# Two-layer token-mixer and expert trunk: the second layer's input rows are scaled and shifted on GpSimd at another place

## The chip, the cores and the metric

One Trainium2 chip, of which the kernel uses one core. The metric is device time in microseconds (us) from start to end of one execution; lower is better. The engines of the core are TensorE (PE in the rows, with its weight loads as PEld), VectorE (DVE), ScalarE (ACT), GpSimd (POOL), and the DMA queues, of which SyncE's (SP) carries nearly all loads here.

## The reference

The batch is 1, the sequence 256 tokens, the width 1024, and there are two layers. Each layer ends both of its halves with a layer normalisation that has a scale row g and a shift row b:

```
mod = silu(c) @ w_ada[l] + b_ada[l]            # six parts: sh_m, sc_m, g_m, sh_f, sc_f, g_f
h   = x * (1 + sc_m) + sh_m
mix = token_mixers(h, w_in[l], w_out[l], ...)  # sparse attention, retention, mLSTM, then @ w_out
x   = layer_norm(alpha * x + (1 + g_m) * mix, ln_mix_g[l], ln_mix_b[l])
h   = x * (1 + sc_f) + sh_f
y   = moe_ffn(h, ...)                          # 16 experts, router, two experts for a token
x   = layer_norm(alpha * x + (1 + g_f) * y, ln_ffn_g[l], ln_ffn_b[l])

layer_norm(x, g, b) = (x - mean) * rsqrt(var + eps) * g + b
```

So the x that enters the second layer is needed twice: in h, ahead of the projections, and in `alpha * x`, behind w_out.

## The kernel before

**Tiles.** The tokens stand as two blocks of 128 on the partitions; a residual tile holds 128 x 2048 numbers (two blocks by 1024). One tile of tag X and three of tag H have that size. Weights come through a ring of ten 128x1024 buffers, rows such as g and b through two buffers of tag row.

**What one layer does.** The function `projections` multiplies h with w_in in eight parts, called projection 0 to 7 (0, the index part, is w_idx, 332 wide). Each goes over eight blocks k of 128 rows of the weight. Work in fp32 precision is done as three products of a high and a low part (`three`, L434 to L436); `wsplit` makes the parts of a weight block: ScalarE's cast (L415) and VectorE's subtraction with two SBUF inputs (L416; L426 has the same form for the first four blocks of projection 0). The parts lie in eight buffers of tag w, so four blocks at once. Between and behind the projections stand the attention's softmax, the convolution and gates of the mLSTM, and the retention's scores. The rope (L523 to L529) leaves one of its halves to GpSimd (L528) and the other to VectorE (L529).

**Places that the change touches.**
- The step between the layers (L880 to L895): the normalised rows xn of the first layer are transposed on TensorE, scaled and shifted by columns into the high part (ScalarE) and a second copy, and L888, a subtraction on VectorE, makes the low part of h. Beside it GpSimd's `affine_rows` (L459 to L466) makes the residual rows from xn: four multiplications by the g row (L463) and four additions of the b row (L464), each 128x512.
- The softmax: L633 on GpSimd divides by the sums.
- `make_aff` (L838): three VectorE operations of 128x8 (L841 to L843) that fold a norm's g and b columns into the modulation's scale and shift. Called ahead of the expert part with the name afff; L935 then makes a router weight of 128x128 from it. The modulation columns come from L406 and L411.
- The retention: scores (L716) into PSUM, masked by VectorE (L791, L792). L772 is the mLSTM's normalisation product, with one input in PSUM and one in SBUF; TensorE's scores wait for its result here.
- w_out is multiplied by (1 + g_m) on GpSimd (L917, 128x512), and split as above.
- L1039 fills the next residual tile with zeros on GpSimd.

**What sets the order.** The instructions of each engine are ordered by a scheduler ahead of time, from the program's order, priorities and dependences; `tc.issue_after(x)` holds an instruction behind x in that order. Loads go out on SyncE's queue in the order in which they are added to a list at the start (`Stream.add`), some 22 ahead of their use.

## Time and profile before

| | |
|---|---|
| Median of three runs | 730.05 us (729.27 to 730.53) |
| Profiled execution | 729.74 us |
| Span of the profile, first to last instruction | 728.0 us |
| Mean granted clock of TensorE | 0.957 of full speed |
| Busy share: TensorE, VectorE, ScalarE, GpSimd | 92%, 57%, 39%, 29% |

The busy share is an average over stages; the granted clock is that of TensorE, 1.00 for 2.4 GHz and 0.50 for 1.2 GHz. All rows of a trace come from the profiled execution.

### The profile page before, as it was taken

Reading aid. Unit: us, or ns where it says so; the run is one execution under the profiler, and the core shown is the slowest. Engines: PE = TensorE matmul, PEld = TensorE weight load, DVE = VectorE, ACT = ScalarE, POOL = GpSimd, SP = SyncE. Lnnn points to the kernel's source line nnn. Section 1 sums busy time; section 2 is a strip of 40 time slices with the busy share of each in tenths; the row PEclk is TensorE's granted clock in tenths of the full one; section 3 lists DMA queues with packets and bytes.
Section 4 is the critical chain, followed back from the end, with each engine's and each line's share of the span. In section 5 each row is a group of like instructions: output and inputs, shape, how many; then the busy total and the mean of one; then the engine's idle time right before and its main releaser. Section 6 shows DMA issues by size and latency. Waiting matters only on the chain. (4 is left out here: it accounts for less than half of the span.)

```text
span 728.0 us, 10437 instructions
## 1 busy us (share of the span) xinstructions
PE 667.6 (92%) x3638; PEld 409.9 (56%) x3638; DVE 414.1 (57%) x903; ACT 280.9 (39%) x583; POOL 208.2 (29%) x195
## 2 busy tenths in 40 slices
PE   5999699999898999999888999999899799999994
PEld 0567587864675434434347678885568554433431
DVE  5478986653975321243477999754645632234245
ACT  3346758344332212122256646944523212222131
POOL 3002933101913046102035613310740303712001
PEclk9999989999897999999998999999969789999998
DMA  8997773499986899999945773439958578999951
GB/s 305 407 368 241 258 267 112 144 363 409 377 299 236 310 322 349 370 408 407 365 156 172 235 256 116 144 125 319 396 183 276 187 264 304 354 353 407 406 193 58
DMA packets 57760, 204.19 MB, mean 280 GB/s; under 512 B 7336, under 2 KB 7464, under 8 KB 56422
## 3 DMA queue, kind: packets, MB, share of 16 engines
q1 hardware_dynamic: 55152, 198.49, 75.5%
q0 software_dynamic: 2112, 4.44, 1.6%
q8 instruction: 30, 0.49, 0.3%
q10 hardware_dynamic: 438, 0.54, 0.2%
q14 instruction: 28, 0.23, 0.1%
HBM read 202.15 MB, written 4.19 MB: 283 GB/s over the span
## 5 line engine op out<-in xcount | busy, mean ns | idle before, releaser
L416 DVE TENSOR_TENSOR sb_w<-sb_ring,sb_w 128x512 fp32r<-128x512 f32 (+1 forms) x156 | 117.1, 764 | 42.6 <-ACT sb_w L415 40.6
L415 ACT CAST sb_w<-sb_ring 128x512 fp32r<-128x512 f32 (+1 forms) x156 | 92.1, 608 | 89.0 <-PE ps_mm L435 44.2
L1208 PE MATMUL ps_s<-sb_ring,sb_S 128*64 128x512 f32 x424 | 116.2, 600 | 0.2 <-PEq L1117 0.2
L435 PE MATMUL ps_mm<-sb_w,sb_H 128*128 128x512 f32 (+2 forms) x224 | 79.9, 359 | 4.3 <-DVE sb_H L888 4.3
L434 PE MATMUL ps_mm<-sb_w,sb_H 128*128 128x512 f32 (+2 forms) x224 | 80.2, 365 | 1.9 <-ACT sb_w L415 1.3
L436 PE MATMUL ps_mm<-sb_w,sb_H 128*128 128x512 f32 (+2 forms) x224 | 74.9, 369 | 0.7 <-DVE sb_w L416 0.6
L917 POOL TENSOR_TENSOR sb_ring<-sb_ring,sb_g 128x512 f32<-128x512 f32 x32 | 45.5, 1460 | 72.0 <-DMA sb_ring<-w_out 70.8
L1208 PEld LDWEIGHTS ps_s<-sb_ring,sb_S 128*64 128x64 f32 x424 | 32.5, 136 | 54.0 <-issue 45.9
L349 PE MATMUL ps_t<-sb_ring,cact 128*32 128x512 f32 x272 | 47.7, 616 | 7.8 <-DVE posf L296 6.2
L434 PEld LDWEIGHTS ps_mm<-sb_w,sb_H 128*128 128x128 f32 x224 | 43.0, 194 | 10.7 <-ACT sb_w L415 2.8
L435 PEld LDWEIGHTS ps_mm<-sb_w,sb_H 128*128 128x128 f32 x224 | 43.3, 194 | 10.1 <-DVE sb_H L888 5.0
L436 PEld LDWEIGHTS ps_mm<-sb_w,sb_H 128*128 128x128 f32 x224 | 41.7, 194 | 11.6 <-issue 3.8
L1107 DVE TENSOR_SCALAR sb_S<-ps_t,afffg,afffb 128x256 f32<-128x256 f32 x32 | 17.4, 543 | 48.9 <-ACT sb_S L210 48.4
L1099 PEld LDWEIGHTS ps_t<-sb_O,sb_H 128*128 128x128 f32 x256 | 33.1, 193 | 19.9 <-issue 11.4
L1256 PE MATMUL ps_t<-sb_P,sb_sg 128*64 128x512 f32 x152 | 42.4, 599 | 0.5 <-ACT sb_sg L1243 0.5
L528 POOL TENSOR_TENSOR sb_rope<-sb_rope 128x256 f32<-128x256 f32 (+1 forms) x16 | 15.8, 990 | 89.3 <-DVE iwm L564 31.5
L435 PE MATMUL ps_mm<-sb_H,sb_w 128*128 128x256 f32 x128 | 37.3, 292 | 3.9 <-DVE sb_w L416 3.9
L1099 PE MATMUL ps_t<-sb_O,sb_H 128*128 128x256 f32 x256 | 39.0, 297 | 2.0 <-DVE sb_O L1029 1.8
L633 POOL TENSOR_SCALAR sb_sg<-sb_sg,sm 128x128 f32<-128x128 f32 (+1 forms) x32 | 26.6, 847 | 45.5 <-DVE sm L630 23.3
L210 ACT ACTIVATE sb_S<-ps_t,afffb,afffg 128x256 f32<-128x256 f32 x32 | 18.0, 563 | 55.9 <-PE ps_t L1099 55.1
L434 PE MATMUL ps_mm<-sb_H,sb_w 128*128 128x256 f32 x128 | 37.1, 291 | 0.0
L436 PE MATMUL ps_mm<-sb_H,sb_w 128*128 128x256 f32 x128 | 36.9, 288 | 0.0
(369 smaller groups left out, 1234.1 us busy)
## 6 DMA issues: line engine op xcount, KB each, us to landing
sb_ring<-w_gu SPq DMA_DIRECT2D x106, 512.0 KB, 7.4
sb_ring<-w_ada SPq DMA_DIRECT2D x96, 512.0 KB, 6.9
sb_P<-w_dn SPq DMA_DIRECT2D x58, 512.0 KB, 7.9
sb_ring<-w_in SPq DMA_DIRECT2D x56, 512.0 KB, 6.1
sb_ring<-w_out SPq DMA_DIRECT2D x16, 512.0 KB, 10.1
sb_S<-w_gu SPq DMA_DIRECT2D x6, 1024.0 KB, 8.4
sb_row<-rows SPq DMA_DIRECT2D x8, 512.0 KB, 9.6
sb_w<-w_gu SPq DMA_DIRECT2D x12, 256.0 KB, 4.7
```

The costliest lines, as they stand in the source:

```text
L210: return A.activation(o, i, f, bias=bias, scale=scale)
L349: PE.matmul(pa[32 * g:32 * g + 32, :], cact[:, k:k + 1].to_broadcast([P, 32]), w[g // 2][:, (g % 2) * 512:(g % 2) * 512 + 512], start=(i = ...
L415: A.copy(hi, src)
L416: V.tensor_tensor(lo, src, hi.bitcast(F32), op=OP.subtract)
L434: PE.matmul(o, a[0], b[0], start=start, stop=False)
L435: PE.matmul(o, a[1], b[0], start=False, stop=False)
L436: return PE.matmul(o, a[0], b[1], start=False, stop=stop)
L633: G.tensor_scalar(sg[:, i * n:(i + 1) * n], sg[:, i * n:(i + 1) * n], sm[:, h:h + 1], None, op0=OP.mult)
L917: G.tensor_tensor(q, q, g1[l][0][:, n * 512:(n + 1) * 512], op=OP.mult)
L1099: last = PE.matmul(pt[:, j * 256:(j + 1) * 256], src[:, tt * D + k * P:tt * D + (k + 1) * P], oh[:, tt * D + q * 256:tt * D + (q + 1) * 25 ...
L1208: PE.matmul(pgu[s * 64:s * 64 + 64, :], xg[:, c0:c0 + 64], ws[s][k], start=(i == order[0] and k == 0), stop=(i == order[3] and k == 1), ti ...
L1256: PE.matmul(pyb[s * 64:s * 64 + 64, :], hdT[:, k, s * 64:s * 64 + 64], wd[s][k], start=(k == 0), stop=(k == 1), tile_position=(0, 64 * s))
```

## The change

In the second layer the residual rows are no longer made at the step between the layers. The normalised rows xn stay in their H tile, and the eight operations of `affine_rows` work in place on it later, behind the softmax's last GpSimd operation (`behind.soft`), issued with projection 5. Their two row loads move in SyncE's list from ahead of w_idx to behind projection 5. The tile that the convolution uses is taken from X in the second layer, and from H in the first as before. Apart from that, in both layers `make_aff` for the expert part is issued behind the last masked retention score (`projections.scored`).

```diff
--- before.py
+++ after.py
@@ -153,13 +153,13 @@
                     st.add(("in", l, n), chunk(l, n), which=(i,))
         for la, na in EARLY[l]:
             st.add(("ada", la, na), w_ada[la, na])
-        if l:
-            norm_rows(2 * l - 1)
         for n in range(8):
             if l or n > 1:
                 st.add(("in", l, n), chunk(l, n))
             for la, na in LATER[l].get(n, ()):
                 st.add(("ada", la, na), w_ada[la, na])
+            if l and n == 5:
+                norm_rows(2 * l - 1)
         norm_rows(2 * l)
         for n, which in ((0, (0, 1)), (1, (0, 1)), (0, (2,)), (1, (2,)), (0, (3,)), (1, (3,))):
             st.add(("out", l, n), w_out[l, n], which=which)
@@ -505,6 +505,9 @@
             if l == 0 and n == 5:
                 with tc.issue_after(st.last.ins):
                     nc.sync.dma_start(xres, x_tok)
+            if l and n == 5:
+                with tc.issue_after(behind.soft.ins):
+                    affine_rows(xres, xres, 2 * l - 1)
             while pending:
                 modulation(*pending.pop(0), ones, "t")
             for la, na in LATER[l].get(n, ()):
@@ -630,7 +633,7 @@
                     V.reciprocal(sm[:, h0:h1], sm[:, h0:h1])
                     for i in range(per):
                         h = h0 + i
-                        G.tensor_scalar(sg[:, i * n:(i + 1) * n], sg[:, i * n:(i + 1) * n], sm[:, h:h + 1], None, op0=OP.mult)
+                        behind.soft = G.tensor_scalar(sg[:, i * n:(i + 1) * n], sg[:, i * n:(i + 1) * n], sm[:, h:h + 1], None, op0=OP.mult)
                     pt = ps("t")
                     for j in range(4):
                         PE.transpose(pt[:, j * P:(j + 1) * P], sg[:, j * P:(j + 1) * P], ident)
@@ -687,7 +690,7 @@
         for k, w in blocks(3):
             cols_part(k, wsplit(w), [pm[j // 2][:, (j % 2) * 256:(j % 2) * 256 + 256] for j in range(4)])
         behind(3)
-        cvs = sb("H").rearrange("p (i j t) -> p i j t", i=2, j=4)
+        cvs = sb("X" if l else "H").rearrange("p (i j t) -> p i j t", i=2, j=4)
         cv, sg = cvs[:, 0], cvs[:, 1]
         mq = sb("S")
         mqk = mq[:, 0:1024].rearrange("p (h t) -> p h t", h=4)
@@ -789,7 +792,7 @@
         rv = sdb[:, 1536:2048].rearrange("p (t d) -> p t d", t=2)
         for h, pq in scores(rqk[:, 0:2, :], rqk[:, 2:4, :]):
             V.tensor_tensor(sd[h][:, 0:256], pq[:, 0:256], dec[:, h, :], op=OP.mult)
-            V.tensor_tensor(sd[h][:, 256:384], pq[:, 256:384], dec[:, h, 0:128], op=OP.mult)
+            projections.scored = V.tensor_tensor(sd[h][:, 256:384], pq[:, 256:384], dec[:, h, 0:128], op=OP.mult)
         pv = ps("mm")
         pv = [pv[:, tt * 256:(tt + 1) * 256] for tt in range(2)]
         pgt = ps("mm")
@@ -891,8 +894,8 @@
                 with tc.issue_after(moved.ins):
                     A.copy(a, sums)
                 modulation(la, na, a, quad, "t", True)
-            xres = sb("X")
-            affine_rows(xres, xn, 2 * l - 1)
+
+            xres = xn
 
         oT = projections(l, hT, inputs)
 
@@ -929,7 +932,8 @@
 
         ws = [(n, j, out_w(n, j)) for n in range(2) for j in (6, 7)]
         st.ahead = AHEAD + 8
-        gp, bp = make_aff(par_("lnm_g")[:, l * 8:l * 8 + 8], par_("lnm_b")[:, l * 8:l * 8 + 8], modc[l][:, 3, :], modc[l][:, 2, :], "afff")
+        with tc.issue_after(projections.scored.ins):
+            gp, bp = make_aff(par_("lnm_g")[:, l * 8:l * 8 + 8], par_("lnm_b")[:, l * 8:l * 8 + 8], modc[l][:, 3, :], modc[l][:, 2, :], "afff")
 
         wrg = wk.tile([P, KD, E], F32, name="wrg", tag="wrg")
         V.tensor_tensor(wrg, wr, gp[:, :, None].to_broadcast([P, KD, E]), op=OP.mult)
```

The next rows give, for one engine each, the program's order of instructions ("x4" is a run of four). On **GpSimd**, second layer, from the end of the expert part of the first layer to w_out's scaling (L453 is a statistic of the norm, L380 a sum for the modulation). A piece of the difference at the step between the layers (rows with a minus stood there before):

```order
 L1161 DMA sb_H<-table_117,which 128x1024 x2
 L453 TENSOR_SCALAR mr<-mv,rs 128x1 x2
-L463 TENSOR_TENSOR sb_X<-sb_H,sb_row 128x512 x4
-L464 TENSOR_TENSOR sb_X<-sb_X,sb_row 128x512 x4
 L380 TENSOR_TENSOR sb_a<-sb_a,sb_ring 128x512 x4
 L531 TENSOR_TENSOR sb_rope<-sb_rope 128x5x32
```

and one behind the softmax (rows with a plus stand there now; lines are numbered 3 to 4 higher after the change, so L636 is L633, L531 is L528, L920 is L917 and L1043 is L1039):

```order
 L636 TENSOR_SCALAR sb_sg<-sb_sg,sm 128x128 x8
 L636 TENSOR_SCALAR sb_sg<-sb_sg,sm 128x256 x8
+L463 TENSOR_TENSOR sb_H<-sb_H,sb_row 128x512 x4
+L1043 MEMSET sb_X 128x2048
+L464 TENSOR_TENSOR sb_H<-sb_H,sb_row 128x512 x4
 L531 TENSOR_TENSOR sb_rope<-sb_rope 128x8x32 x2
 L920 TENSOR_TENSOR sb_ring<-sb_ring,sb_g_3715 128x512 x16
-L1043 MEMSET sb_X 128x2048
```

The eight row operations moved from behind the norm to behind the softmax, work on sb_H in place, and have the zero fill of the next sb_X between them; the rope's halves of projection 5 stand behind them.

On **VectorE**, second layer, at the retention's scores. Before:

```order
L406 TENSOR_REDUCE mod<-ps_t 128x4
L411 TENSOR_TENSOR modc_269<-mod,bada 128x2x2
L841 TENSOR_TENSOR afffg<-pr,modc_269 128x8
L842 TENSOR_TENSOR afffb<-pr,modc_269 128x8
L772 TENSOR_TENSOR sb_e<-ps_s,sb_e 128x512
L935 TENSOR_TENSOR wrg<-pr,afffg 128x128
L843 TENSOR_TENSOR afffb<-afffb,modc_269 128x8
L791 TENSOR_TENSOR sb_S<-ps_s,dec 128x256
L792 TENSOR_TENSOR sb_S<-ps_s,dec 128x128
L791 TENSOR_TENSOR sb_S<-ps_s,dec 128x256
L792 TENSOR_TENSOR sb_S<-ps_s,dec 128x128
```

and now (L772 in it is L769 of before; the product that was L772 is L775 and stands four rows further up, straight behind L411):

```order
L795 TENSOR_TENSOR sb_S<-ps_s,dec 128x128
L772 TENSOR_TENSOR sb_O<-sb_e,sb_O 128x512
L794 TENSOR_TENSOR sb_S<-ps_s,dec 128x256
L795 TENSOR_TENSOR sb_S<-ps_s,dec 128x128
L794 TENSOR_TENSOR sb_S<-ps_s,dec 128x256
L795 TENSOR_TENSOR sb_S<-ps_s,dec 128x128
L844 TENSOR_TENSOR afffg<-pr,modc_269 128x8
L845 TENSOR_TENSOR afffb<-pr,modc_269 128x8
L939 TENSOR_TENSOR wrg<-pr,afffg 128x128
L846 TENSOR_TENSOR afffb<-afffb,modc_269 128x8
L416 TENSOR_TENSOR sb_w<-sb_ring,sb_w 128x512 x4
```

The three operations of `make_aff` and the router product moved from both sides of L772 (now L775) to behind the last masked score, ahead of the splits of w_out.

On **VectorE**, first layer (affmg and affmb are the parts for the step to the second layer, which have stood among the retention's scores already). Before, ahead of the mLSTM's scores:

```order
L406 TENSOR_REDUCE mod<-ps_t 128x4
L411 TENSOR_TENSOR modc_268<-mod,bada 128x2x2
L841 TENSOR_TENSOR afffg<-pr,modc_268 128x8
L842 TENSOR_TENSOR afffb<-pr,modc_268 128x8
L935 TENSOR_TENSOR wrg<-pr,afffg 128x128
L843 TENSOR_TENSOR afffb<-afffb,modc_268 128x8
L721 TENSOR_TENSOR sb_P<-ps_s,sb_P 128x384
```

and now, at the end of the retention's scores:

```order
L795 TENSOR_TENSOR sb_S<-ps_s,dec 128x128
L845 TENSOR_TENSOR affmb<-pr,modc_269 128x8
L794 TENSOR_TENSOR sb_S<-ps_s,dec 128x256
L795 TENSOR_TENSOR sb_S<-ps_s,dec 128x128
L844 TENSOR_TENSOR afffg<-pr,modc_268 128x8
L845 TENSOR_TENSOR afffb<-pr,modc_268 128x8
L846 TENSOR_TENSOR affmb<-affmb,modc_269 128x8
L939 TENSOR_TENSOR wrg<-pr,afffg 128x128
L846 TENSOR_TENSOR afffb<-afffb,modc_268 128x8
L416 TENSOR_TENSOR sb_w<-sb_ring,sb_w 128x512 x4
```

The afff operations left the place between two L721 and stand between those of affm, directly ahead of the splits of w_out.

On TensorE the order changes at one place of the stretch: in the second layer the transposes of the rope's result of projection 5 (L785) stand eight to eighteen matmuls of the next projections later.

## Rows read from the trace of the kernel before

**Rows 1.** The page, busy us, share of the span and instructions of each engine:

```profile
PE 667.6 (92%) x3638; PEld 409.9 (56%) x3638; DVE 414.1 (57%) x903; ACT 280.9 (39%) x583; POOL 208.2 (29%) x195
```

**Rows 2.** Timeline of GpSimd, 330 to 640 (start us, length, operation, idle before):

```profile
375.93 5.68 POOL L463 TENSOR_TENSOR sb_X<-sb_H,sb_row 128x512 f32<-128x512 f32 x4 [0.32 <-DVE sb_H L1289]
381.57 5.84 POOL L464 TENSOR_TENSOR sb_X<-sb_X,sb_row 128x512 f32<-128x512 f32 x4
...
463.83 4.75 POOL L633 TENSOR_SCALAR sb_sg<-sb_sg,sm 128x256 f32<-128x256 f32 x4 [2.53 <-DVE sm L630]
478.65 1.58 POOL L528 TENSOR_TENSOR sb_rope<-sb_rope 128x256 f32<-128x256 f32 x1 [10.08 <-DVE rowz L661]
...
566.51 1.80 POOL L1039 MEMSET sb_X<- 128x2048 f32 x1 [30.40 <-DVE sb_H L835]
```

**Rows 3.** VectorE's groups, 375.9 to 387.4 (count, busy us, mean ns, idle before):

```profile
L888 DVE TENSOR_TENSOR sb_H<-sb_h,sb_H 128x256 fp32r<-128x256 f32 x4 | 5.3, 1342 | 0.0
L426 DVE TENSOR_TENSOR sb_w<-sb_ring,sb_w 128x332 fp32r<-128x332 f32 x4 | 5.2, 1288 | 0.0
```

**Rows 4.** VectorE's groups, 388 to 394:

```profile
L416 DVE TENSOR_TENSOR sb_w<-sb_ring,sb_w 128x332 fp32r<-128x332 f32 x4 | 2.0, 493 | 0.0
L888 DVE TENSOR_TENSOR sb_H<-sb_h,sb_H 128x256 fp32r<-128x256 f32 x4 | 1.7, 421 | 0.1
```

**Rows 5.** TensorE's waits, 374 to 400 (total us, times, longest):

```profile
PE ps_mm L435 <- DVE sb_H L888: 4.3, 2, 2.4
```

**Rows 6.** Windows: length, then busy us (count) by engine; granted clock last but two:

```profile
382.00:388.00 6.00, 3.55 (x13) 3.17 (x12) 6.00 (x5) 1.63 (x4) 5.41 (x4) 0.50 0.32 111
...
468.00:482.00 14.00, 14.00 (x101) 12.65 (x99) 12.98 (x26) 7.18 (x13) 3.12 (x3) 1.00 0.66 217
482.00:488.00 6.00, 6.00 (x50) 5.53 (x49) 0.00 (x0) 3.99 (x10) 0.00 (x0) 1.00 0.05 21
526.00:538.00 12.00, 10.76 (x26) 7.38 (x28) 6.39 (x13) 1.75 (x3) 10.11 (x8) 0.50 0.53 193
```

**Rows 7.** Timeline, second layer's retention scores, 518 to 548:

```profile
523.55 1.02 DVE L411 TENSOR_TENSOR modc<-mod,bada 128x4 f32<-128x4 f32 x1
524.61 1.19 DVE L841 TENSOR_TENSOR afffg<-pr,modc 128x8 f32<-128x8 f32 x1
...
525.80 0.68 DVE L772 TENSOR_TENSOR sb_e<-ps_s,sb_e 128x512 f32<-128x512 f32 x1
...
526.53 1.65 PE L716 MATMUL ps_s<-sb_S 64*128 64x256 f32 x4 [2.88 <-DVE sb_e L772]
527.08 1.22 DVE L843 TENSOR_TENSOR afffb<-afffb,modc 128x8 f32<-128x8 f32 x1
...
528.89 1.64 PE L716 MATMUL ps_s<-sb_S 64*128 64x256 f32 x4 [0.71 <-DVE sb_S L792]
```

**Rows 8.** Timeline of VectorE, first layer, 138 to 215:

```profile
151.55 0.17 DVE L841 TENSOR_TENSOR afffg<-pr,modc 128x8 f32<-128x8 f32 x1
...
187.25 1.82 DVE L416 TENSOR_TENSOR sb_w<-sb_ring,sb_w 128x512 fp32r<-128x512 f32 x1
```

**Rows 9.** VectorE's groups, first layer's w_out stretch, 179.4 to 204:

```profile
L416 DVE TENSOR_TENSOR sb_w<-sb_ring,sb_w 128x512 fp32r<-128x512 f32 x8 | 11.6, 1458 | 0.6 <-ACT sb_w L415 0.6
```

**Rows 10.** Timeline of TensorE, projection 6 of the second layer:

```profile
471.61 0.75 PE L436 MATMUL ps_mm<-sb_w,sb_H 128*128 128x512 f32 x3
...
477.71 0.28 PE L436 MATMUL ps_mm<-sb_w,sb_H 128*128 128x256 f32 x1
```

**Rows 11.** Timeline of VectorE, 455 to 500:

```profile
469.97 1.27 DVE L416 TENSOR_TENSOR sb_w<-sb_ring,sb_w 128x512 fp32r<-128x512 f32 x2
...
474.59 0.67 DVE L416 TENSOR_TENSOR sb_w<-sb_ring,sb_w 128x512 fp32r<-128x512 f32 x1
...
479.24 0.40 DVE L529 TENSOR_TENSOR sb_rope<-sb_rope 128x256 f32<-128x256 f32 x1
```

**Rows 12.** Timeline of TensorE, first layer's w_out stretch, 176 to 216:

```profile
190.81 1.02 PE L436 MATMUL ps_mm<-sb_w,sb_O 128*128 128x512 f32 x2
```

## The prediction

> **What bounds the kernel now.** Lines are those of the kernel before (the same lines stand 3 or 4 further down after the change). I read the page first: TensorE is busy for 92% of the span and no other engine for more than 57% [rows 1], so time is gained or lost where TensorE waits or runs at the lower clock. The change touches four stretches, and I looked at each by its own view.
>
> At the step between the layers GpSimd runs the eight row operations of the scale and shift from 375.93 to 387.41 [rows 2]. In that stretch VectorE's subtractions with two SBUF inputs take 1342 and 1288 ns [rows 3]; the same shapes take 421 and 493 ns just behind it [rows 4]. TensorE waits 4.3 us for those subtractions [rows 5], and from 382 to 388 it runs at 0.50 of the clock, 1.2 GHz [rows 6].
>
> Behind the softmax, from 468 to 482, TensorE is busy 14.00 of 14.00 us at full clock and VectorE 12.98 of 14, while GpSimd works 3.12 us [rows 6]. This is where the row operations go: free for GpSimd, full for the two others.
>
> At the retention scores of the second layer VectorE's tiny operations take about 1.2 us each while GpSimd scales w_out, and TensorE waits 2.88 us for the operation behind them [rows 7]. TensorE then runs at 0.50 until 538 [rows 6]. In the first layer the same tiny operations stand in a quiet place, at 0.17 us [rows 8].
>
> **The change part by part.** All four sums use one mechanism, which the rows show: while GpSimd runs a chain of operations with SBUF inputs, a VectorE operation with two SBUF inputs gets in about once per GpSimd operation, whatever its size. In the w_out stretches 128x8 elements cost 1.19 us [rows 7] and 128x512 cost 1.46 us on average [rows 9], while L772, which has one input in PSUM, stays at 0.68 us there [rows 7]. I call one turn a slot, of 1.46 us (5.84 for four GpSimd operations [rows 2]).
>
> *Step between layers.* Eight GpSimd operations leave. VectorE's eight subtractions there shrink by 4 x (1.342 - 0.421) + 4 x (1.288 - 0.493) = 6.9 us [rows 3, 4]. TensorE's 4.3 us of waiting should mostly go [rows 5], and of its 3.55 us busy at half clock half is saved, 1.8 us [rows 6]: 6.1 together. Next in line are ScalarE's two activations for each block, which TensorE and VectorE also need, so some waiting stays, about 1 us as I estimate from following the chain with the short durations. I take a gain of 5.0. Bounds: 6.9, all of VectorE's saving; and 3.0, the wait less 1.3 for what ScalarE holds back, with the clock falling all the same. The two row loads leave the queue ahead of w_idx; nothing waited for that queue here, so I price it at nothing; if it did count, it would be a gain of the two issues.
>
> *Behind the softmax.* The softmax's last GpSimd operation ends at 468.58 [rows 2]. Then come four multiplications, the zero fill of the next residual tile (1.80 us, now between them [rows 2]) and four additions: 8 x 1.46 + 1.80 = 13.5 us, to about 482.1. Counted along VectorE's order, the operations with two SBUF inputs are: the last split of projection 5, one gate operation, the splits of blocks 0 and 1 of projection 6 (slots 1 to 4); the splits of blocks 2 and 3 (under the fill); two gate operations and the split of block 4 (slots 5 to 7). Block 0 is then split by 468.58 + 3 x 1.46 + 0.67 = 473.6. TensorE wants it with the third matmul of the row at 471.61, about 472.0 [rows 10]; before, it was there ahead of that, being the first of the pair at 469.97 [rows 11]. TensorE waits 1.6 us. Block 4 is split by 468.58 + 4 x 1.46 + 1.80 + 3 x 1.46 + 0.67 = 481.3 in place of 475.26 [rows 11]; TensorE wants it at 477.71 [rows 10], now 479.3: another 2.0. After that GpSimd is done and VectorE catches up, as it is idle from 482 to 488; TensorE is not, 6.00 of 6.00 [rows 6], so what it lost stays lost. The loss is 3.6 us. Bounds: 1.0, if the splits are far enough ahead for most of it; 7, if a fall of the clock comes on top (the second rival).
>
> The fill is priced as if it did not contend. No row shows a fill beside such a VectorE operation. If it took slots like a reader, blocks 2 and 3 would be late too, by at most one slot on the path, 1.5 us; if it does not, nothing. I take nothing, since L772 shows that it is the second SBUF read that is held up [rows 7], and a fill reads nothing. The Trainium skill, page "SBUF — State Buffer", section "Who interferes with whom", says the same outright: a VectorE instruction with two SBUF inputs contends with a GpSimd instruction that reads SBUF and not with one that only writes. By that rule the loss here is the 3.6 of the slots; by a rule that all GpSimd work contends it would be 5.1, and the sum below -0.6 in place of -2.1. No row of this trace decides it.
>
> Queued behind the row operations on GpSimd is the rope's half for projection 5, which started at 478.65 [rows 2] and now starts about 3.5 us later. TensorE's transposes wait for it; the new order puts them behind eight to eighteen more matmuls, and TensorE itself is 3.6 late by then, so I add nothing. Without that cover it would be up to 3.5 us. The row loads now go out between the weights of projections 5 and 6, so ahead of weights that are already split at 469.97 [rows 11]; the next row loads, which need the same two buffers, go out only behind the weights of projection 7. No wait for either. The convolution's tile moves from H to X, which is free since the residual was folded in near the end of the first layer: no wait. The fill leaves its place ahead of the token split, where GpSimd had stood idle for 30.40 us before it [rows 2]; what follows it there can only come earlier: nothing.
>
> *Affine parts, second layer.* L411 ends at 524.57. L772 could start then, but starts at 525.80 behind L841 (1.19) [rows 7]. Without those it starts 1.2 us earlier, and TensorE's scores at 526.53 come at 525.3. The next scores, at 528.89, waited for L791 and L792, which stood behind L843 (1.22, from 527.08) and the router product [rows 7]; they now follow at once, at about 527.0. With the bank that the last scores need free as well, TensorE is 2.4 us ahead by then (1.2 + 0.7 of the second wait + about 0.5 of the third). The four operations themselves go behind the last score, where VectorE next waits for ScalarE: free. Gain 2.4. Bounds: 1.2, the first wait alone; 4.3, if the stretch at half clock gets shorter too.
>
> *Affine parts, first layer.* The same four leave a quiet place (0.17 us, [rows 8]) for one inside the w_out stretch, directly ahead of the split at 187.25 [rows 8]. In the second layer they took slots of 1.19 and 1.22 [rows 7], and two more squeezed into the same gaps; here I take two slots less the gap they fill, 2.5 us. The split that ended at 189.07 then ends at 191.6, and TensorE wants it at 190.81 [rows 12]: 0.8 of waiting at first, up to 2.5 where later operations in the chain have no slack. I take a loss of 1.7, the middle. Bounds: 0 and 4.8 (four at 1.19).
>
> **Sum.** -5.0 + 3.6 - 2.4 + 1.7 = -2.1 us. The profiled execution took 729.74 us (span 728.0 and 1.7 around it), 0.3 below the median of 730.05; its sum gives 727.6, and against the median 728.0.
>
> **Rivals.**
> *The window hides more* (T = 725.4): the splits run far enough ahead and the loss behind the softmax is 1.0. For it: eight buffers hold four pairs, and beside a single GpSimd operation, the rope's half at 478.65, VectorE's L529 took 0.40 while GpSimd's took 1.58 [rows 2, 11], so it can be GpSimd that is held up. Against: the row operations come in chains of four, as at the step, and the split of block 0 is only about one block ahead of its use [rows 10, 11]. Sum -5.0 + 1.0 - 2.4 + 1.7 = -4.7.
> *Slower: the clock falls behind the softmax* (T = 732). Two waits of 1.6 and 2.0 us in a stretch that was gapless. At the step, waits of 4.3 in all were followed by the lower clock [rows 5, 6], and in 526 to 538 TensorE was busy 10.76 us at 0.50 [rows 6]. A fall to 1.2 GHz costs half of the busy time it lasts. It makes the change slower than before by 0.2% from 3.6 us of loss on, which is 7 us at the lower clock; for 8 us it costs 4.0 and the sum is +1.9. Against it: the two waits are five us apart with dense work between.
> *The step gives less* (T = 730.0): ScalarE's activations or the lower clock hold the step; the gain is 3.0, the sum -0.1. For it: ScalarE is the next in that chain. It is also the case in which the move does not do what it is for.
>
> **How the numbers follow.** Forecast 0.52, window hidden 0.13, clock falls 0.20, step gives less 0.15. Within 0.2%, 1.46 us, a measurement of this kernel can hardly tell a difference from none. Faster: most of the forecast (0.43) and the hidden window (0.13): 0.56. Slower: most of the third case, 0.18. Same: the rest, 0.26. The range reaches from below the hidden window, 724.8, to inside the slower case, 731.6; the forecast alone would be 726.0 to 729.4.
>
> **What would show it.** Right: at the step L888 near 0.42 us, no wait of TensorE over 1 us, full clock; behind the softmax L416 near 1.5 us and two waits of TensorE for it, 3 to 4 us in all; in the second layer's scores the product of L772 straight behind L411 and the wait down to about 1.7; in the first layer four operations of 0.2 to 1.2 us ahead of the split. Wrong: granted clock below 1 between 470 and 490; TensorE waiting at the step for ScalarE; a wait of TensorE for GpSimd's rope.

## The result

The changed kernel took 723.17 us (median of 20 runs, 718.45 to 727.46) against 728.2 us for the kernel before (median of 20, 726.15 to 733.25). The ratio is 0.9927, with a 95% interval of 0.9906 to 0.9947: 5.3 us faster, 3.9 to 6.9. The direction was as forecast; the size forecast was 2.1 us. The median lies below the stated range (724.8). Some of that is the reference: the three runs of the kernel before that were shown had a median of 730.05, the twenty have 728.2. The rest, 5.3 in place of 2.1 us, is the change itself. The ratios here and below leave out runs that lie more than 1.5% above the fastest of their kernel: three of twelve in r4, one of six in r13, and one of the 17 of the kernel before beside r12 to r14.

The profile after, for the lines that answer to [rows 1, 2, 5]. The page, busy us and share of the span by engine; GpSimd's timeline from 455 to 495; TensorE's waits from 374 to 400; and a window at the step (columns as in [rows 6]):

```profile
PE 669.7 (92%) x3638; PEld 407.6 (56%) x3638; DVE 414.8 (57%) x903; ACT 280.5 (39%) x583; POOL 212.5 (29%) x195
```

```profile
467.57 8.51 POOL L463 TENSOR_TENSOR sb_H<-sb_H,sb_row 128x512 f32<-128x512 f32 x4
476.02 1.81 POOL L1043 MEMSET sb_X<- 128x2048 f32 x1
477.79 7.51 POOL L464 TENSOR_TENSOR sb_H<-sb_H,sb_row 128x512 f32<-128x512 f32 x4
485.26 0.90 POOL L531 TENSOR_TENSOR sb_rope<-sb_rope 128x256 f32<-128x256 f32 x1
```

```profile
PE ps_mm L434 <- ACT sb_H L210: 0.6, 1, 0.6
PE ps_mm L436 <- DVE sb_w L416: 0.6, 1, 0.6
PE ps_mm L435 <- DVE sb_H L891: 0.5, 1, 0.5
```

```profile
382.00:388.00 6.00, 4.92 (x31) 4.23 (x32) 5.37 (x13) 5.92 (x14) 0.00 (x0) 1.00 0.97 370
```

The page hardly moves. At the step the 4.3 us of waiting for VectorE's subtractions [rows 5] are down to 0.5, the two other waits are short (0.6 each), and TensorE has the full clock. Behind the softmax the row operations take 8.51 and 7.51 us for four, where they took 5.68 and 5.84 at the step [rows 2], and the rope's half starts at 485.26.

**Lengths of stretches.** To compare many kernels I measured each stretch between two landmarks that all have: the ends of VectorE's 160 splits of weights from the ring (L416 and L426), numbered from 0 in its order. The names r1 to r14 are those of the experiments below. *First w_out* is from split 62 to 78, *step* from 80 to 84, *softmax* from 126 to 136, *scores* (second layer, with half of its w_out) from 136 to 152, and *last* from split 158 to the end of the span. In us, from one profile each:

| Kernel | First w_out | Step | Softmax | Scores | Last | Span |
|---|---|---|---|---|---|---|
| before | 46.9 | 10.5 | 31.1 | 52.6 | 168.1 | 728.0 |
| before, again (r8) | 45.9 | 10.5 | 31.4 | 52.2 | 168.1 | 728.5 |
| changed | 49.6 | 4.9 | 35.3 | 47.2 | 167.7 | 725.6 |
| changed, again (r1) | 50.1 | 4.9 | 35.2 | 47.1 | 166.5 | 723.8 |
| changed, third (r11) | 49.6 | 4.9 | 35.1 | 48.8 | 166.8 | 722.2 |
| r2 rows only | 46.8 | 4.9 | 34.6 | 51.4 | 166.7 | 721.3 |
| r3 rows, second affine | 45.9 | 4.9 | 35.3 | 47.5 | 166.7 | 719.4 |
| r4 affine only | 49.6 | 10.5 | 31.1 | 48.2 | 168.0 | 727.0 |
| r9 second affine only | 45.9 | 10.5 | 31.1 | 46.3 | 169.0 | 721.9 |
| r10 first affine only | 49.6 | 10.5 | 31.5 | 51.1 | 169.1 | 729.7 |
| r12 second fill late | 45.8 | 10.5 | 31.6 | 52.1 | 167.0 | 723.5 |
| r5 rows behind rope | 46.7 | 4.9 | 31.3 | 45.5 | 166.8 | 712.8 |
| r6 rows left out | 45.8 | 4.9 | 31.7 | 47.5 | 166.9 | 716.1 |
| r7 one input | 45.8 | 4.9 | 32.4 | 42.5 | 166.5 | 710.8 |

Mean of the changed kernel's three profiles less the mean of the two of before: +3.4, -5.7, +4.0, -4.7 and -1.1, together -4.1; the spans differ by -4.4. Four of these are the terms of the prediction. The fifth, the last part, it had at nothing. What moves the span of one kernel from run to run lies mostly outside these stretches: in the sixteen profiles the time up to split 62 is 162.7 to 166.3 us, and that from split 78 to 80, the first layer's expert part, 164.4 to 167.7 (160.7 in r13).

### The profile page after: what moved, and what is told of

Read it like the earlier page. It is cut to its first block, busy times and chain, and to the rows that moved or that the text cites. A ratio compares the mean times of both kernels' runs of the same rounds, so it can differ in the third digit from the quotient of the medians.

```text
span 725.6 us, 10434 instructions
## 1 busy us (share of the span) xinstructions
PE 669.7 (92%) x3638; PEld 407.6 (56%) x3638; DVE 414.8 (57%) x903; ACT 280.5 (39%) x583; POOL 212.5 (29%) x195
## 5 line engine op out<-in xcount | busy, mean ns | idle before, releaser
L416 DVE TENSOR_TENSOR sb_w<-sb_ring,sb_w 128x512 fp32r<-128x512 f32 (+1 forms) x156 | 116.6, 761 | 40.2 <-ACT sb_w L415 39.1
L920 POOL TENSOR_TENSOR sb_ring<-sb_ring,sb_g 128x512 f32<-128x512 f32 x32 | 45.9, 1473 | 69.7 <-DMA sb_ring<-w_out 39.2
L1212 PEld LDWEIGHTS ps_s<-sb_ring,sb_S 128*64 128x64 f32 x424 | 32.8, 137 | 55.3 <-issue 47.1
L436 PEld LDWEIGHTS ps_mm<-sb_w,sb_H 128*128 128x128 f32 x224 | 41.1, 192 | 14.3 <-DVE sb_w L416 5.2
L434 PEld LDWEIGHTS ps_mm<-sb_w,sb_H 128*128 128x128 f32 x224 | 42.6, 191 | 10.0 <-issue 2.7
L435 PEld LDWEIGHTS ps_mm<-sb_w,sb_H 128*128 128x128 f32 x224 | 42.8, 191 | 6.0 <-DVE sb_H L891 0.9
L1260 PE MATMUL ps_t<-sb_P,sb_sg 128*64 128x512 f32 x152 | 44.0, 622 | 0.5 <-ACT sb_sg L1247 0.5
L435 PE MATMUL ps_mm<-sb_H,sb_w 128*128 128x256 f32 x128 | 38.1, 298 | 2.9 <-DVE sb_w L416 2.9
L636 POOL TENSOR_SCALAR sb_sg<-sb_sg,sm 128x128 f32<-128x128 f32 (+1 forms) x32 | 26.4, 842 | 47.0 <-DVE sm L633 24.9
L531 POOL TENSOR_TENSOR sb_rope<-sb_rope 128x256 f32<-128x256 f32 (+1 forms) x16 | 14.9, 931 | 78.5 <-DVE iwm L567 30.8
L434 PE MATMUL ps_mm<-sb_H,sb_w 128*128 128x256 f32 x128 | 37.8, 297 | 0.0
L436 PE MATMUL ps_mm<-sb_H,sb_w 128*128 128x256 f32 x128 | 37.8, 295 | 0.0
```

Of the source, the lines that this page charges most:

```text
L416: V.tensor_tensor(lo, src, hi.bitcast(F32), op=OP.subtract)
L434: PE.matmul(o, a[0], b[0], start=start, stop=False)
L435: PE.matmul(o, a[1], b[0], start=False, stop=False)
L436: return PE.matmul(o, a[0], b[1], start=False, stop=stop)
L636: behind.soft = G.tensor_scalar(sg[:, i * n:(i + 1) * n], sg[:, i * n:(i + 1) * n], sm[:, h:h + 1], None, op0=OP.mult)
L920: G.tensor_tensor(q, q, g1[l][0][:, n * 512:(n + 1) * 512], op=OP.mult)
```

## The experiments

Time ratios are to the kernel before on the same chip; a ratio of 0.001 is 0.73 us.

**r1, r11: the changed kernel again.** No edit.

> The changed kernel once more, for a second profile. Theory A (the four stretches of the prediction, with the sizes that the first profile shows: first layer's affine parts +2.7 us, step -5.9, behind the softmax +4.2, second layer's scores -5.6): each stretch moves by the same amount to within 0.5 us, and the ratio to the kernel before is again 0.990 to 0.995. Rival B (one of the stretches has two outcomes, and the median lies at the better one): the profiled execution lands some 5 us lower than the first (722 instead of 727), and one stretch shows a different wait or a different granted clock.

> The changed kernel a third time, for a third profile. Theory A: the four stretches as in the first two profiles to within 1 us (step 4.9 us, softmax 35.2, second layer's scores 47.2, first layer's w_out 49.8); what differs from them stands elsewhere, in how long the granted clock is low. Rival B: an execution below 722 us is one in which one of the four stretches is 2 us shorter.

Ratio 0.9912 (0.9882 to 0.9942) in r1; r11 is one run, of 723.86 us. The four stretches came out alike in three profiles, the scores within 1.7 us and the others within 0.6. That speaks against rival B, but no profiled execution was below 722 us, so what such a run does differently stays open.

**r2: the row operations alone.**

```diff
-        with tc.issue_after(projections.scored.ins):
+        with nullcontext():
             gp, bp = make_aff(par_("lnm_g")...
```

> Only the row operations are moved behind the softmax; both make_aff stand where they stood in the kernel before. Theory A: step -5.9 and softmax +4.2 stay, the two terms of make_aff (+2.7 and -5.6) go, so 1.7 us below the kernel before, 2.9 above the changed kernel. Rival C (what is lost behind the softmax is given back at w_out, because w_out's loads and GpSimd's scaling of it set the end of that stretch): about 5 us below the kernel before, and the delay of +3 us in the splits ahead of w_out is gone behind them without make_aff having moved.

Ratio 0.9962 (0.9939 to 0.9986), -2.8 us. The scores stretch stays at 51.4, so the delay from the softmax isn't given back there. Theory A's -1.7 lies inside the interval (-4.4 to -1.0); C's -5 does not.

**r3: the row operations, and make_aff moved in the second layer only.**

```diff
-        with tc.issue_after(projections.scored.ins):
+        with tc.issue_after(projections.scored.ins) if l else nullcontext():
```

> The changed kernel with the first layer's make_aff left where it stood before; the second layer's is behind the scores. Theory A: the loss of 2.7 us among the first layer's splits of w_out goes, so 2.7 us below the changed kernel (2 to 4, if the expert part passes it on), about 7 below the kernel before. Rival D (the first layer's delay is hidden by the loads of the expert part): the same time as the changed kernel within 0.7 us.

Ratio 0.9850 (0.9812 to 0.9888), median 718.3 against 722.1 for the changed kernel beside it. D is out: the first layer's move costs the changed kernel some 4 us. The -10.9 (-13.7 to -8.2, from five runs) is more than r2 and r9 (below) add up to, -7.9; the span of the profile is 719.4. Why stays open.

**r4, r9, r10: make_aff alone, in both layers, in the second, in the first.** The row operations stay at the step.

```diff
+        with tc.issue_after(projections.scored.ins):                            # r4
+        with tc.issue_after(projections.scored.ins) if l else nullcontext():      # r9
+        with tc.issue_after(projections.scored.ins) if not l else nullcontext():  # r10
             gp, bp = make_aff(par_("lnm_g")...
```

> Only make_aff is moved behind the scores, in both layers; the row operations stay at the step. Theory A: +2.7 and -5.6, so 2.9 us below the kernel before, with TensorE's 4.3 us of waiting at the step unchanged. Rival C (the -5.6 at the second layer's scores is mostly the given-back delay of the softmax and not make_aff): within 1 us of the kernel before or up to 1 us above it.

> The kernel before with nothing changed but make_aff of the second layer behind the scores. Theory A (this term is worth 4 to 5 us and not the 2.4 of the prediction, since the stretch at the lower clock behind it gets shorter too): the stretch from the last splits of projection 7 to the third block of w_out falls from 52.4 to 47.5 us, the time by 4 to 5 us, and the lower clock lasts some 7 us there in place of 13.7. Rival H (its price is the 2.4 of the two waits, and the rest of what the changed kernel gains there is given-back delay of the softmax): the stretch at 50, the time 2 to 2.5 us lower.

> The kernel before with nothing changed but make_aff of the first layer behind the scores. Theory A: the stretch from the last split of projection 7 to the last of w_out in the first layer grows from 46.2 (mean of seven profiles) to 49.7 us, and the time by 3 to 3.5. Rival I (the loss is 1.7 as predicted, and the expert part's loads give some of it back): 0 to 1.7 us slower.

Ratios 0.9963 (0.9930 to 0.9995), 0.9930 (0.9905 to 0.9955) and 1.0034 (1.0012 to 1.0055): -2.7, -5.1 and +2.5 us. The second and third together with r2's -2.8 add up to -5.4, the whole change being -5.3. H is out: the second layer's move is worth 5.1 by itself. I (0 to 1.7) is not excluded by the time alone (0.9 to 4.0), but by the stretch, which is 49.6 to 50.1 in the five profiles with the move and 45.8 to 46.9 in the nine of the table without. r4's -2.7 matches the sum of r9 and r10 but is no check of it: it rests on nine of twelve runs, the mean of all twelve is 0.7 us below the kernel before, and the two medians (728.58 and 728.52) are alike. So r4 alone decides nothing between A and C; r9 does.

**r5, r14: the row operations behind the rope.** As r3, with this in place of the call behind the softmax:

```diff
             A.copy(rqk[:, :, tt * P:(tt + 1) * P], ...)
+        if l:
+            with tc.issue_after(rope.last.ins):     # the rope's last GpSimd operation
+                affine_rows(xres, xres, 2 * l - 1)
```

> As the run with the second layer's affine parts alone, but the eight row operations stand behind the rope's last GpSimd operation of projection 5, where VectorE was idle for 6 us and half idle behind, in place of straight behind the softmax. Theory A (the loss behind the softmax is VectorE being held up by the row operations): the stretch from the last splits of projection 4 to the first of projection 7 falls from 35.3 to 31.1 us, and the time by 4 us below that run, to about 1.020 below the kernel before in per cent terms 2.0. Rival E (wherever the row operations go in this layer they cost 3 to 4 us, to another user of two SBUF inputs or to w_out): within 1 us of that run.

> The run with the row operations behind the rope again, to stand beside the run with the late fill on one chip: 0.980 to 0.985 of the kernel before, by either theory.

Ratios 0.9823 (0.9799 to 0.9848) and 0.9832 (0.9802 to 0.9862). The softmax stretch is 31.3 and 31.7, and neither the scores nor the last part is longer than in r3, so the stretches bear out theory A. GpSimd's timeline of r5, 440 to 520:

```profile
475.03 4.97 POOL L463 TENSOR_TENSOR sb_H<-sb_H,sb_row 128x512 f32<-128x512 f32 x4
479.97 4.98 POOL L464 TENSOR_TENSOR sb_H<-sb_H,sb_row 128x512 f32<-128x512 f32 x4
```

In a quiet place one row operation takes 1.24 us; behind the softmax it took 2.13. The medians (715.75 and 717.4 against r3's 718.3) show less than the 4 us of the stretch, and the intervals of r3 and r5 overlap, so against r3 the time alone does not exclude E. Against the kernel before, the two are -12.9 and -12.3 us; r9 (-5.1), the step (-5.7) and the fill (-1.1 to -2.1, r12 below) add up to -11.9 to -12.9, with nothing lost behind the softmax.

**r6: the row operations cut to 8 columns.**

```diff
-                    affine_rows(xres, xres, 2 * l - 1)
+                    G.tensor_tensor(xres[:, 0:8], xres[:, 0:8], rowt[0][:, 0:8], op=OP.mult)
+                    G.tensor_tensor(xres[:, 0:8], xres[:, 0:8], rowt[1][:, 0:8], op=OP.add)
```

> As the run with the second layer's affine parts alone, but the row operations cover 8 of 1024 columns only: the rest of the scale and shift of the second layer's residual rows is left out. Bound for the cost of the row operations in that place. Theory A: the same stretch at 31.0 to 31.4 us, 4 us below that run, and GpSimd's rope half of projection 5 early again. Rival F (the loss comes from the row loads between the weights, not from GpSimd's operations): the stretch stays near 35.

The softmax stretch is 31.7 with the row loads still between the weights, so the loads do not make the loss and F is out. The ratio, 0.9852 (0.9826 to 0.9878), is no lower than r3's 0.9850: the 4 us that were expected do not show in the time. Other residual rows can send other tokens to the second layer's experts, but the last part is as long as r3's (166.9 and 166.7), so that is not shown to be the reason. I rest on the stretch alone here.

**r7: the same eight operations with one input tile.** The call of `affine_rows` is replaced by its loop with these operations; the scale and shift by rows is left out.

```diff
-                G.tensor_tensor(q, xn[:, o], t[0][:, c0:c0 + 512], op=OP.mult)
-                G.tensor_tensor(q, q, t[1][:, c0:c0 + 512], op=OP.add)
+                G.tensor_scalar(q, q, rowt[0][:, c0:c0 + 1], None, op0=OP.mult)
+                G.tensor_scalar(q, q, rowt[1][:, c0:c0 + 1], None, op0=OP.add)
```

> As the run with the second layer's affine parts alone, but the eight row operations multiply by or add one number per partition, so that each has one SBUF tile to read in place of two; the scale and shift by rows is left out. GpSimd is as long busy, and the rope's half of projection 5 stands behind it as before. Theory A in the narrow form (it is GpSimd's two-input operations that hold up VectorE; the softmax's own division, with one input, left splits beside it at 0.68 us): the gate operations behind the softmax return to 0.4 to 0.7 us, the splits stay at 0.67, and of the 4.2 us at most 1 to 1.5 stays, for the rope. Theory A in the wide form (any read of SBUF by GpSimd holds VectorE up): the gate operations stay at 1.5 us or more and the loss at about 4. Rival G (the loss is GpSimd's queue, the rope's half being late): the loss stays at 4 with short gate operations.

GpSimd is as busy (16.4 us for the eight), the ratio is 0.9768 (0.9743 to 0.9793), and the stretch is 32.4: 1.2 over the kernels before, in place of 4.0. Two timelines of VectorE around the gate operations, of the changed kernel first and of r7 below:

```profile
468.06 1.39 DVE L416 TENSOR_TENSOR sb_w<-sb_ring,sb_w 128x512 fp32r<-128x512 f32 x1
469.37 1.51 DVE L653 SCALAR_TENSOR_TENSOR sb_rope<-sb_rope 4x256 f32<-4x256 f32 x1
470.81 1.27 DVE L416 TENSOR_TENSOR sb_w<-sb_ring,sb_w 128x512 fp32r<-128x512 f32 x2
472.01 0.27 DVE L656 TENSOR_SCALAR sb_rope<-sb_rope 4x256 f32<-4x256 f32 x1
472.21 1.28 DVE L416 TENSOR_TENSOR sb_w<-sb_ring,sb_w 128x512 fp32r<-128x512 f32 x2
473.42 1.50 DVE L657 TENSOR_TENSOR sb_rope<-sb_rope 4x256 f32<-4x256 f32 x1
474.95 1.67 DVE L658 TENSOR_TENSOR_SCAN sb_rope<-sb_rope 4x256 f32<-4x256 f32 x1
...
477.13 0.67 DVE L416 TENSOR_TENSOR sb_w<-sb_ring,sb_w 128x512 fp32r<-128x512 f32 x1
```

```profile
462.79 0.41 DVE L658 SCALAR_TENSOR_TENSOR sb_rope<-sb_rope 4x256 f32<-4x256 f32 x1
...
464.32 0.69 DVE L661 TENSOR_SCALAR sb_rope<-sb_rope 4x256 f32<-4x256 f32 x1
...
466.14 0.41 DVE L662 TENSOR_TENSOR sb_rope<-sb_rope 4x256 f32<-4x256 f32 x1
...
471.81 1.07 DVE L668 TENSOR_SCALAR rowz<-sb_rope 4x256 f32<-4x256 f32 x1
```

L653 and L657 are L658 and L662 of r7: 1.51 and 1.50 us beside GpSimd operations with two inputs, 0.41 beside operations with one. So the narrow form holds for what VectorE's operations take. The stretch is a weaker witness: in r7 TensorE's order is another from the rope's transposes on. They stand behind all gate rows, at 481.99, where GpSimd's half had ended at 480.50, and waited for nothing. So r7 does not show what the late rope (G) costs where the transposes stand earlier; that is the wait of 1.1 us shown further down. The Trainium skill, page "SBUF — State Buffer", section "Who interferes with whom", has a VectorE instruction with two SBUF inputs contend with any GpSimd instruction that reads SBUF; r7 shows that one-input reads left these at 0.41, and the measurement decides.

**r8: the kernel before again.**

> The kernel before once more, for a second profile. Theory A: the four stretches have the lengths of the first profile to within 0.5 us (step 10.5 us, softmax 31.1, second layer's scores 52.6), and what differs between the two executions stands at other places, where the granted clock falls for a longer or a shorter time. Rival B: one of the four stretches itself varies by 2 us or more.

One run, of 731.14 us. Its stretches repeat (first w_out differs by 1.0, the others by 0.4 or less); the first layer's expert part differs by 1.9.

**r12, r13: the zero fill held behind the token split.** r12 is the kernel before with this edit in the second layer, r13 is r5 with it in the first.

```diff
-            G.tensor_tensor(xl[:, o], xn[:, o], ...)
+            low = G.tensor_tensor(xl[:, o], xn[:, o], ...)
...
-        G.memset(xrow, 0.0)
+        with tc.issue_after(low.ins) if l else nullcontext():   # r12
+        with nullcontext() if l else tc.issue_after(low.ins):   # r13
+            G.memset(xrow, 0.0)
```

> The kernel before with nothing changed but the zero fill of the second layer's residual tile, held behind the two subtractions of the token split on GpSimd. Theory J (the fill, which the change took out of this place as a side effect, holds up VectorE's normalisation beside it: 2.49 us in place of 0.81): the first normalisation at 0.81 us, the part from the last split of w_out to the end 1.2 to 1.7 us shorter (168.1 to 166.6), and the time by as much. Rival K (the prediction's: the fill lies in idle time there and costs nothing; the shorter last part in the runs with moved rows has another cause): the last part at 168, the time within 0.5 us of the kernel before.

> As the run with the row operations behind the rope, and the first layer's zero fill held behind the token split too. Theory J: the first normalisation of the first layer falls from 2.49 to 0.81 us, and the time by up to 1.7 us, if the expert part of the first layer passes it on. Rival K: no change, within 0.5 us.

r12: 0.9971 (0.9950 to 0.9992), -2.1 us, and the last part 167.0 in place of 168.1. In all profiles with the second layer's fill in its old place the last part is 168.0 to 169.1, in all others 166.5 to 167.7. VectorE's timeline around the norm that follows w_out, of the kernel before, the changed one (here with the second normalisation too) and r12:

```profile
566.37 2.49 DVE L957 TENSOR_SCALAR sb_H<-sb_H,mv,rs 128x1024 f32<-128x1024 f32 x1
```

```profile
564.28 0.81 DVE L961 TENSOR_SCALAR sb_H<-sb_H,mv,rs 128x1024 f32<-128x1024 f32 x1
...
567.15 2.00 DVE L961 TENSOR_SCALAR sb_H<-sb_H,mv,rs 128x1024 f32<-128x1024 f32 x1
```

```profile
562.96 0.81 DVE L957 TENSOR_SCALAR sb_H<-sb_H,mv,rs 128x1024 f32<-128x1024 f32 x1
```

The fill of 1.80 us started at 566.51 [rows 2], 0.14 behind L957, and L957 took 2.49. With the fill elsewhere it takes 0.81. TensorE's waits, of the kernel before and of r12:

```profile
PE ps_t L850 <- DVE sb_H L957: 2.0, 2, 1.4
```

```profile
PE ps_t L850 <- DVE sb_H L957: 0.6, 1, 0.6
```

Theory J holds. It is not the fill alone that does this: the second normalisation, which runs beside GpSimd's token split (2.35 us, from 566.25 in the changed kernel), still takes 2.00, and 2.03 in the kernel before.

r13: 0.9805 (0.9773 to 0.9837) against r14's 0.9832 on the same chip. Its first normalisation fell from 2.49 to 0.81 too, but the two ratios cannot be told apart. In its one profile the first layer's expert part takes 160.7 us, against 164.4 to 167.7 in the fifteen others; whether the fill does that is not shown.

## Why the prediction was right or wrong

**Step between the layers: right.** 5.0 forecast, 5.7 found, in every kernel without the row operations there. The subtractions, with columns as in [rows 3] and from the same window:

```profile
L426 DVE TENSOR_TENSOR sb_w<-sb_ring,sb_w 128x332 fp32r<-128x332 f32 x4 | 2.0, 499 | 0.5 <-ACT sb_w L424 0.5
...
L891 DVE TENSOR_TENSOR sb_H<-sb_h,sb_H 128x256 fp32r<-128x256 f32 x4 | 1.6, 421 | 0.1
```

They are at 499 and 421 ns, and from 382 to 388 TensorE ran at full clock (1.00), so the rival in which the step gives less did not happen.

**Behind the softmax: size right by luck, path mostly wrong.** 3.6 forecast, 4.0 found. The prediction had VectorE get one two-input operation in for each GpSimd operation, whatever its size. Beside the first four row operations (467.57 to 476.08) it got eight in: four took 1.39 to 1.67 us, and four splits in two pairs took 0.64 each. So the splits hardly paid (the first took 1.39), and the tiny gate operations took a turn of 1.5 us or more each. GpSimd paid as well, at 2.13 and 1.88 us for an operation in place of the 1.46 that I took, so the eight and the fill took 17.7 us and not 13.5. That late end hit what I had priced at nothing, the rope; a wait for it was one of the signs by which I wanted to know that I was wrong. TensorE's waits from 464 to 492, and two windows (columns as in [rows 6]):

```profile
PE ps_t L788 <- DVE sb_rope L526: 1.1, 1, 1.1
PE ps_mm L436 <- DVE sb_w L416: 0.7, 2, 0.4
PE ps_s L675 <- DVE rowz L663: 0.5, 1, 0.5
```

```profile
476.00:482.00 6.00, 5.20 (x36) 4.27 (x35) 6.00 (x9) 1.59 (x3) 6.00 (x5) 1.00 0.42 138
482.00:488.00 6.00, 4.76 (x34) 4.10 (x35) 5.29 (x8) 1.95 (x5) 5.13 (x4) 1.00 0.35 116
```

Splits 0.7 in place of the 3.6 forecast, a gate row 0.5, and 1.1 for the transposes of the rope (L788). These are 2.3 of the 4.0 us by which the stretch grew; for the rest I have no row. The row names L526, which does not feed them; GpSimd's half, which does, ended at 486.16 and the transposes began at 486.21. The clock stayed at 1.00, so the rival in which it falls here did not happen, and nor did the one in which the buffers hide the delay. The sub-step on the fill held here: L416 at 477.13 took 0.67 beside it.

**The fill's old place: wrong.** "What follows it there can only come earlier: nothing." I looked at what waits behind the fill on GpSimd, and not at who works beside it. VectorE's normalisation did, and TensorE's transposes waited for it. The term is -1.1 us in the profiles and -2.1 (-0.6 to -3.6) in r12. The Trainium skill, page "SBUF — State Buffer", section "Who interferes with whom", says, besides the sentence that I weighed, that a VectorE tensor_scalar can enter a mode with two ports and that this and GpSimd then shut each other out for a whole instruction. The 2.49 and 2.00 against 0.81 agree with it, and I had drawn on the sentence about two-input operations alone; whether the normalisation ran in that mode no run here shows.

**Second layer's affine parts: the step that failed most.** 2.4 forecast with a bound of 4.3; 4.7 in the profiles and 5.1 (3.3 to 6.9) in r9. The step that failed is the clock: I summed the waits and left the time at the lower clock as it was. The waits did what I said. The changed kernel's timeline there, answering to [rows 7]:

```profile
525.99 1.03 DVE L411 TENSOR_TENSOR modc<-mod,bada 128x4 f32<-128x4 f32 x1
...
526.94 0.68 DVE L775 TENSOR_TENSOR sb_e<-ps_s,sb_e 128x512 f32<-128x512 f32 x1
...
527.67 1.45 PE L719 MATMUL ps_s<-sb_S 64*128 64x256 f32 x8 [1.33 <-DVE sb_e L775]
```

The product stands straight behind L411, the first wait fell from 2.88 to 1.33 and the second is gone: 2.3 us. What I kept for the bound only, a shorter time at the lower clock, came on top. The eight scores from 527.67 on took 1.45 us at full clock, where four took 1.65 and 1.64 before [rows 7]. In the 12 us from the second scores on, TensorE ran at 0.50 before [rows 6]. The same 12 us of the changed kernel and of r9:

```profile
527.00:539.00 12.00, 11.33 (x54) 8.51 (x55) 8.15 (x17) 2.45 (x4) 12.00 (x9) 0.72 0.76 270
```

```profile
524.00:536.00 12.00, 11.75 (x62) 8.86 (x62) 9.54 (x17) 3.50 (x6) 12.00 (x9) 0.86 0.79 274
```

As an estimate, at 0.72 and 0.86 the 10.76 busy us of before hold 10.76 x 0.22 = 2.4 and 10.76 x 0.36 = 3.9 us more work at full speed. In the profiles my term lacked 2.3 us for the changed kernel and 3.7 for r9 (52.4 to 46.3, less 2.4); by r9's timed runs it lacked 2.7.

The other profiles let the two parts be told apart. TensorE's waits ahead of the second and third scores, the granted clock of the 12 us from the second scores on, and the stretch, in us:

| Profile | Waits | Clock | Scores |
|---|---|---|---|
| before | 2.88, 0.71 | 0.50 | 52.6 |
| r2, no edit here | 2.70, 0.94 | 0.57 | 51.4 |
| r10, no edit here | 3.02, 0.71 | 0.59 | 51.1 |
| r11, changed | 1.95, none | 0.60 | 48.8 |
| changed | 1.33, none | 0.72 | 47.2 |
| r9 | 1.29, none | 0.86 | 46.3 |
| r5 | 1.58, none | 1.00 | 45.5 |

At nearly the same clock (0.57 to 0.60) the stretch is 2.3 to 2.6 us shorter with the short waits: about the 2.4 of my term. The rest goes with the clock. One program, the changed kernel, had 0.72, 0.72 and 0.60 in its three profiles, so the order alone does not fix it. But every profile with this edit has 0.60 or more and a scores stretch of 48.8 or less, every one without it 0.59 or less and 51.1 or more (r7 is left out of this, as the work behind its scores came in another order). That the shorter waits are what keeps the time at the lower clock short is inferred from this; no run sets the clock by itself.

**First layer's affine parts: mis-sized.** 1.7 forecast, 3.4 in the profiles, 2.5 (0.9 to 4.0) in r10. VectorE's and TensorE's timelines of the changed kernel:

```profile
186.83 1.30 DVE L845 TENSOR_TENSOR afffb<-pr,modc 128x8 f32<-128x8 f32 x1
188.06 1.33 DVE L846 TENSOR_TENSOR affmb<-affmb,modc 128x8 f32<-128x8 f32 x1
189.31 1.42 DVE L939 TENSOR_TENSOR wrg<-pr,afffg 128x128 f32<-128x128 f32 x1
190.65 1.23 DVE L846 TENSOR_TENSOR afffb<-afffb,modc 128x8 f32<-128x8 f32 x1
191.80 5.75 DVE L416 TENSOR_TENSOR sb_w<-sb_ring,sb_w 128x512 fp32r<-128x512 f32 x4
```

```profile
192.53 0.73 PE L436 MATMUL ps_mm<-sb_w,sb_O 128*128 128x512 f32 x2 [2.44 <-DVE sb_w L416]
```

I let two of the four slip into gaps; only the first did, at 0.78 us (186.13). Here each of the others took its turn, and the split that began at 187.25 before [rows 8] began at 191.80 (0.7 of that is from ahead of this stretch).

So the mechanism, turns between GpSimd and VectorE, held at the step and in both w_out stretches, and behind the softmax only in part. The sum was off by 3.2 us. By the timed runs that is 2.7 for the second layer's term (the clock) and 1.4 for moving the row operations (-2.8 in r2 where I had -1.4; the fill is the larger part of it), less 0.8 for the first layer.

## What to carry to other kernels

Before moving a GpSimd operation, list what runs on VectorE beside both its old and its new place, zero fills and tiny operations too: in the first layer's w_out stretch a turn cost 1.2 to 1.4 us for 128x8 and 128x128, and 1.4 for 128x512. Put a chain of GpSimd operations with two inputs where VectorE is idle, and not only where GpSimd is: here that choice decided some 4 us of the softmax stretch, of which r5 and r14 against r3 show 1 to 3 in the time. Where a wait stands ahead of a stretch at the lower clock, price the clock as well as the wait. Undo the parts one at a time; two of the five parts of this change worked against the rest. Leaving the first layer's affine parts where they were and putting the row operations behind the rope gave 0.9823 and 0.9832 of the time before, with the first layer's fill late 0.9805.

## What the runs showed of the hardware that was not expected

Both sides pay when GpSimd and VectorE meet: GpSimd's 128x512 operation with two inputs took 1.24 us alone (r5), 1.42 to 1.46 at the step [rows 2] and 1.88 to 2.13 behind the softmax. Turns are not one for one: behind the softmax eight of VectorE's two-input operations got in beside four of GpSimd's, four of them at 0.64 us. A fill of 1.80 us left a two-input subtraction at 0.67 us, but took a one-input normalisation of 128x1024 from 0.81 to 2.49; GpSimd's subtraction of 128x1024 took the same normalisation to 2.00. GpSimd operations with one input left two-input gate operations at 0.41 in r7. VectorE's tiny one-input operations are mixed: 4x256 took 0.27 beside a two-input operation (L656), 0.69 beside a one-input one (L661 of r7), and 1.07 beside the fill (L668 of r7, which began while the fill ran from 470.94 to 472.74).
